# Block-sum transfers of a hybrid encoder layer moved from SyncE to GpSimd, and two stores made one

## The chip, the cores and the metric

One core of a Trainium2 chip runs the whole program. The time is the device time of one execution in microseconds; the median of the runs counts. All times that follow are in us.

## The reference

One encoder layer runs on two sequences (1024 and 2048 tokens of width 1024), each with 16 learned meta tokens ahead. Cut to what matters:

```
xn = rmsnorm(h, g_pre)
proj = xn @ w_in + b_in                      # 1024 -> 6672 columns
na_q, na_k, na_v, na_z, ml_qk, ml_v, ml_z, ml_o, ml_g, mg = split(proj)
ya = (neighbourhood_attention(na_q, na_k, na_v, na_rpb) * silu(na_z)) @ w_a
yb = (mlstm_both_directions(ml_qk, ml_v, ml_g, ml_o, ...) * silu(ml_z)) @ w_b
ga, gb = split(sigmoid(mg))
out = h + rmsnorm((ga * ya + gb * yb) @ w_out, g_post)
```

Inputs and outputs are float32, and so is the arithmetic.

## The kernel before

**Split products.** Each large product is made of float32r parts: a matrix is split into a high part (ScalarE's copy) and a low part (VectorE's subtraction of it), and a product takes three matmuls: high by high, high by low, low by high. Weights arrive in units of 128x1024; each becomes a pair `whi`, `wlo` in one of four buffers (`NBW`). The first time a unit is used it is loaded raw (`wraw`, L274), split, used, and both parts are stored to DRAM (L331); later uses load the two parts again (L296).

**Order of the work.** `PLAN` lists groups of projection columns by sequence and half: mLSTM, attention and gate columns of sequence 0 and of the two halves of sequence 1, then the final projections. The order of TensorE's instructions is written out by the program; the attention and the mLSTM of a sequence are interleaved with projections, so that TensorE always has a projection to work on. VectorE, ScalarE, GpSimd and SyncE are ordered by the scheduler, which goes by a simulated timeline. Each of the engines works its own list in that order; a transfer is issued by an instruction on one engine's list, and when that instruction waits (for its data, or for a semaphore), all that stands behind it on that engine waits too. SyncE issues nearly all transfers: loads of weights and of kept x, stores of projections, their reloads (`raw`, `va`, `um`), and the stores of kept weights.

**Block products.** For gate columns, and for the first twelve columns of the attention, pairs of 128 columns are computed by a seven-product (Strassen) scheme. Its inputs are block sums of weights and of x, made ahead, split in two parts each, and kept in DRAM:

- `wprep` (L564) makes the sums of weights of the eight pairs of gate columns. For each pair it loads two raw units into `pr` (L576), makes four pairs of sums in turn on VectorE, splits them with ScalarE and VectorE into `po`, and stores each sum (L594). `pr` and `po` have one buffer each.
- `nprep` (L600) does the same for the six pairs of attention columns, in tiles `xr` of a pool with four buffers: loads at L608, stores of the two parts of each sum at L623 and L624.
- `tprep` (L627) makes sums of x: `t0` to `t3`, each as a high and a low DRAM tile of 128x4x512, in four steps `e`. A step holds all four `xr` buffers. `t0` and `t1` are the two halves of one SBUF tile, and are made at once. For sequence 0 it also stores the scaled x itself (L653, `xkept`). The sums are stored at L667, a transfer of 128x512 for each sum, part and step.

These three are generators. `beside()` (L546), called after each piece of a projection, advances each of them every second to fourth turn, and ties the next piece behind VectorE's, ScalarE's and SyncE's last instructions of the projection, so that the sums are made in between. All of it runs in the first 1084 us of the profile. The readers come later: `tload` (L917) loads `t0` to `t3`, and the weight pump (L289) loads the sums of weights, both on SyncE; a semaphore makes them wait for the stores.

**Other lists.** GpSimd has 100 short instructions in the profile and a few transfers: the clearing of borders of `raw` (L1415), `st` and `ss` for the mLSTM, copies of meta keys, and loads of bias masks into `kx` (L1183), which ScalarE reads at L1192. Of the mLSTM, L1428 and L1503 are VectorE's convolution rows and the scaled key `kf`, which TensorE transposes at L1539; `L1520` is VectorE's scaling of values. The rows `pj` at L776 to L778 are projections whose stationary operand is a weight, those at L202 to L204 are those with x stationary or weight moving, all of them waiting for `whi` and `wlo`.

Of the kernel before, what the change touches and what calls it, by code (L numbers as in the profile page):

```python
# [10 lines left out]
F32 = mybir.dt.float32  # L11
# [7 lines left out]
P = 128  # L19
TCARGS = dict(schedule_with_timeline_sim=True)  # L20
D = 1024
# [32 lines left out]
PAIRS = [tuple(c[2 * p:2 * p + 2]) for c in (N_COLS, FM_COLS[24:]) for p in range(len(c) // 2)]  # L54
# [3 lines left out]
def _weight_units():  # L58

    return ([("i", x, P) for x in FM_COLS] + [("t", *c, a) for c in TM_COLS for a in range(2)]  # L60
            + [("m", f, P) for f in range(KT)] + [("o", c, a) for c in range(4) for a in range(2)])
# [76 lines left out]
class K:  # L138
# [425 lines left out]
    def wprep(self):  # L564

        nc = self.nc
        unit = {k: j for j, k in enumerate(_weight_units())}
        sub = lambda o, a, b: nc.vector.tensor_tensor(o, a, b, op=ALU.subtract)
        self.pq = ExitStack()
        pool = self.pq.enter_context(self.tc.tile_pool(name="pq", bufs=1, side="right", reuse_waits="tile"))  # L570
        for p in range(6, 14):
            if p == 10:
                [x for x in self.sides if x[0] is self.wside][0][1] = 4
            raw = pool.tile([P, 2, 2, 512], F32, name="pr", bufs=1)
            for f in range(2):
                nc.sync.dma_start(raw[:, f].rearrange("p a c -> p (a c)"), self.i["wu"][unit["i", PAIRS[p][f], P], :, :D])  # L576
            yield
            yield
            for f, ops in ((0, ("11", "12")), (1, ("21", "22")), (1, ("s3", "s1")), (0, ("s2", "s4"))):
                if ops[0] == "s3":  # L580
                    nc.vector.tensor_tensor(raw[:, 1, 1], raw[:, 1, 0], raw[:, 1, 1], op=ALU.add)
                    sub(raw[:, 1, 0], raw[:, 0, 0], raw[:, 1, 0])
                    yield
                if ops[0] == "s2":
                    sub(raw[:, 0, 0], raw[:, 1, 1], raw[:, 0, 0])
                    sub(raw[:, 0, 1], raw[:, 0, 1], raw[:, 0, 0])
                    yield
                o = pool.tile([P, 2, 2, 512], F32R, name="po", bufs=1)
                c = slice(p > 7 and ops[0] == "21", 2)
                nc.scalar.activation(o[:, c, 0], raw[:, f, c], AF.Copy)  # L590
                sub(o[:, c, 1], raw[:, f, c], o[:, c, 0].bitcast(F32))
                for q, op in list(enumerate(ops))[c]:
                    d = self.qd[p, op] = self.dp.tile([P, D], F32, name=f"q{p}{op}")
                    nc.sync.dma_start(d[:, :], o[:, q].rearrange("p a c -> p (a c)").bitcast(F32))  # L594
                yield
                yield
                if ops[0] == "11":
                    yield

    def nprep(self):  # L600

        nc = self.nc
        unit = {k: j for j, k in enumerate(_weight_units())}
        op = lambda o, a, b, x=ALU.subtract: nc.vector.tensor_tensor(o, a, b, op=x)
        for p in range(6):
            r0, r1 = [self.bp.tile([P, 2, 512], F32, name="xr", bufs=4) for _ in range(2)]
            for f, r in enumerate((r0, r1)):
                nc.sync.dma_start(r.rearrange("p a c -> p (a c)"), self.i["wu"][unit["i", PAIRS[p][f], P], :, :D])  # L608
            for _ in range(2):
                yield  # L610
            op(r1[:, 1], r1[:, 0], r1[:, 1], ALU.add)
            op(r1[:, 0], r0[:, 0], r1[:, 0])
            yield
            op(r0[:, 0], r1[:, 1], r0[:, 0])
            op(r0[:, 1], r0[:, 1], r0[:, 0])
            yield
            for r, ops in ((r1, ("s3", "s1")), (r0, ("s2", "s4"))):
                hi = self.bp.tile([P, 2, 512], F32, name="xr", bufs=4)
                nc.scalar.activation(hi.bitcast(F32R), r, AF.Copy)
                op(r.bitcast(F32R), r, hi)  # L620
                for q, o in enumerate(ops):
                    d = self.qd[p, o] = self.dp.tile([P, D], F32, name=f"q{p}{o}")
                    nc.sync.dma_start(d[:, :512], hi[:, q])  # L623
                    nc.sync.dma_start(d[:, 512:], r[:, q])  # L624
                yield

    def tprep(self, s, t0, after):  # L627

        nc, dp = self.nc, self.dp
        tt = lambda o, a, b, op=ALU.subtract: nc.vector.tensor_tensor(o, a, b, op=op)  # L630
        self.TD[s, t0] = [[dp.tile([P, 4, 512], F32, name=f"t{j}{part}{s}{t0}") for part in "hl"] for j in range(4)]
        td = self.TD[s, t0]
        while len(self.xs) < 2 or self.turn < after:
            yield
        if s == 0:
            for a in range(2):
                self.xkept[s, t0 + 512 * a] = [dp.tile([P, KT, 512], F32, name=f"x{part}{s}_{t0 + 512 * a}") for part in "hl"]
        halves = [[x[:, :, b:b + 512].bitcast(F32) for x in y] for y, b in zip(self.xs, (0 if s else NM, 0))]
        for e in range(4):
            ks = slice(2 * e, 2 * e + 2)  # L640
            r0, r1, ta, hi = [self.bp.tile([P, 2, 512], F32, name="xr", bufs=4) for _ in range(4)]
            for a, (r, (h, l)) in enumerate(zip((r0, r1), halves)):
                tt(r, h[:, ks], l[:, ks], ALU.add)
                if s == 0:
                    tt(r, r, self.rr[:, a:a + 1].to_broadcast([P, 2, 512]), ALU.mult)
                yield
            if s == 0:
                for a, r in enumerate((r0, r1)):
                    nc.scalar.activation(hi.bitcast(F32R), r, AF.Copy)
                    tt(ta.bitcast(F32R), r, hi)  # L650
                    for d, x in zip(self.xkept[s, t0 + 512 * a], (hi, ta)):
                        nc.sync.dma_start(d[:, ks, :], x)
                    yield  # L653
                    yield
            tt(ta[:, 0], r1[:, 0], r0[:, 0])
            tt(ta[:, 1], r1[:, 1], ta[:, 0])
            yield
            tt(r1[:, 0], r1[:, 1], r1[:, 0])
            tt(r0[:, 1], r0[:, 1], ta[:, 1])
            yield  # L660
            todo = [(hi, ta, (0, 1)), (r1[:, 1], r1[:, 0], (2,)), (r0[:, 0], r0[:, 1], (3,))]
            for a, b, js in todo:
                nc.scalar.activation(a.bitcast(F32R), b, AF.Copy)
                tt(b.bitcast(F32R), b, a)
                for q, j in enumerate(js):
                    for d, x in zip(td[j], (a, b)):
                        nc.sync.dma_start(d[:, e, :], x[:, q] if len(js) > 1 else x)  # L667
                yield


# [1492 lines left out]
```

## Time and profile before

| what | value |
|---|---|
| median of 3 runs | 2709.54 us (2709.08 to 2713.91) |
| profiled execution: its own time | 2707.9 us |
| its span | 2706.1 us |
| granted TensorE clock, mean | 0.992 |
| busy: TensorE, weight load, VectorE, ScalarE, GpSimd | 2647.0, 2336.6, 1943.8, 1439.9, 16.2 us |
| moved by DMA | 805.75 MB, mean 298 GB/s |
| queue q1 (SyncE), q0 (GpSimd) | 800.04 MB and 87.9%, 2.69 MB and 0.4% of the 16 DMA engines' time |

The span runs from the first to the last instruction of the profiled execution; its own time is 1.8 us longer. "Busy" counts the time in which an engine works on an instruction. The share of a DMA queue is the time that its packets took, as a share of the span of all 16 DMA engines. A row of a wait reads "who and where <- what it waited for". In a row of windows stand the window, its length, then busy time and count for TensorE, weight load, VectorE, ScalarE and GpSimd, then the granted clock, the DMA share and GB/s.

### The profile page before, as it was taken

The page shows a single profiled execution, that of the slowest core. Times are in us where ns is not written, and L with a number is a line of the kernel's source. Part 1 is how long each engine was busy: PE and PEld are TensorE (multiplying, and loading weights), DVE is VectorE, ACT ScalarE, POOL GpSimd, SP SyncE. Part 2 cuts the span into 40 slices and gives each one's busy share as a digit, 9 for nine tenths or more (in the row PEclk, how much of TensorE's full clock was granted, in tenths as well). Part 3 has the DMA queues.
Part 4 walks back from the last instruction along what each step waited for, and adds up shares of the span by engine and source line. Part 5 has one row for each costly group of instructions (what it writes and reads, how often), then busy time and mean ns, then how long its engine had stood idle before and what let it go on. Part 6 is the DMA issues. An engine that isn't in the chain of part 4 may idle for free.

```text
span 2706.1 us, 47482 instructions
## 1 busy us (share of the span) xinstructions
PE 2647.0 (98%) x15928; PEld 2336.6 (86%) x15928; DVE 1943.8 (72%) x5266; ACT 1439.9 (53%) x3388; POOL 16.2 (1%) x100
## 2 busy tenths in 40 slices
PE   9999899998999999999999999999999999999998
PEld 7998798898987999887888888888889998989888
DVE  5655588787766888545686776867478989898954
ACT  5433456554444655555665566656365666656521
POOL 0000000000000000000000000000000000000000
PEclk9999899998999999999999999999999999999999
DMA  9899886899978899878889998899899898898965
GB/s 366 336 342 335 309 306 233 299 336 327 348 228 285 294 320 314 274 265 276 259 271 332 370 297 264 279 331 363 274 305 314 259 309 278 282 305 260 324 238 203
DMA packets 411651, 805.75 MB, mean 298 GB/s; under 512 B 52016, under 2 KB 180992, under 8 KB 409104
## 3 DMA queue, kind: packets, MB, share of 16 engines
q1 hardware_dynamic: 410288, 800.04, 87.9%
q0 software_dynamic: 1120, 2.69, 0.4%
q8 instruction: 126, 2.06, 0.3%
q14 instruction: 117, 0.96, 0.1%
HBM read 548.96 MB, written 253.60 MB: 297 GB/s over the span
## 4 chain that ended last, share of the span: by engine, by line
PE 82%; DMA 9%; DVE 5%; ACT 2%; issue 1%; SPq 1%; DVEq 0%; ACTq 0%
PE pj L202 9%; PE pj L204 9%; PE pj L203 9%; PE pj L971 7%; PE pj L973 7%; PE pj L972 7%; PE pj L776 4%; PE pj L777 4%; PE pj L778 4%; PE pj L1918 3%; PE pj L1919 3%; PE pj L1920 3%; PE sm L1266 3%; PE tr L1251 2%; DMA wraw<-wu 2%
## 5 line engine op out<-in xcount | busy, mean ns | idle before, releaser
L202 PE MATMUL pj<-xh,whi 128*128 128x512 f32 (+1 forms) x896 | 345.5, 386 | 1.0 <-ACT whi L303 0.9
L204 PE MATMUL pj<-xh,wlo 128*128 128x512 f32 (+1 forms) x896 | 337.4, 377 | 5.7 <-DMA wlo<-wl 5.4
L203 PE MATMUL pj<-xl,whi 128*128 128x512 f32 (+1 forms) x896 | 337.9, 377 | 0.1
L776 PE MATMUL pj<-whi,xh 128*128 128x256 f32 (+1 forms) x1152 | 330.9, 287 | 6.8 <-DMA whi<-wh 6.8
L777 PE MATMUL pj<-wlo,xh 128*128 128x256 f32 (+1 forms) x1152 | 326.2, 283 | 3.7 <-DMA wlo<-wl 3.7
L778 PE MATMUL pj<-whi,xl 128*128 128x256 f32 (+1 forms) x1152 | 325.9, 283 | 0.0
L776 PEld LDWEIGHTS pj<-whi,xh 128*128 128x128 f32 x1152 | 218.6, 190 | 7.4 <-DMA whi<-wh 7.0
L777 PEld LDWEIGHTS pj<-wlo,xh 128*128 128x128 f32 x1152 | 218.3, 190 | 4.1 <-DMA wlo<-wl 4.0
L1918 PE MATMUL pj<-whi,mh 128*128 128x256 f32 x768 | 219.8, 286 | 0.5 <-DMA whi<-wh 0.5
L778 PEld LDWEIGHTS pj<-whi,xl 128*128 128x128 f32 x1152 | 218.3, 189 | 0.0
L1920 PE MATMUL pj<-whi,mlo 128*128 128x256 f32 x768 | 216.6, 282 | 0.0
L1919 PE MATMUL pj<-wlo,mh 128*128 128x256 f32 x768 | 216.6, 282 | 0.0
L204 PEld LDWEIGHTS pj<-xh,wlo 128*128 128x128 f32 x896 | 170.9, 191 | 38.8 <-DMA wlo<-wl 6.2
L202 PEld LDWEIGHTS pj<-xh,whi 128*128 128x128 f32 x896 | 170.9, 191 | 30.8 <-ACT whi L303 1.8
L203 PEld LDWEIGHTS pj<-xl,whi 128*128 128x128 f32 x896 | 170.9, 191 | 27.5 <-issue 1.0
L1258 DVE TENSOR_TENSOR pts<-tr,pts 96x384 fp32r<-96x384 f32 (+2 forms) x192 | 118.5, 617 | 57.2 <-ACT pts L1253 55.3
L1253 ACT ACTIVATE pts<-tr 96x384 fp32r<-96x384 f32 (+2 forms) x192 | 103.5, 539 | 98.8 <-PE tr L1251 98.1
L202 PE MATMUL pj<-yh,whi 128*128 128x512 f32 x384 | 154.4, 402 | 0.0
L203 PE MATMUL pj<-yl,whi 128*128 128x512 f32 x384 | 150.9, 393 | 0.8 <-DVE yl L1820 0.8
L204 PE MATMUL pj<-yh,wlo 128*128 128x512 f32 x384 | 151.1, 394 | 0.0
L1918 PEld LDWEIGHTS pj<-whi,mh 128*128 128x128 f32 x768 | 145.4, 189 | 1.5 <-DMA whi<-wh 0.7
L1919 PEld LDWEIGHTS pj<-wlo,mh 128*128 128x128 f32 x768 | 145.5, 189 | 0.8
(368 smaller groups left out, 6962.5 us busy)
## 6 DMA issues: line engine op xcount, KB each, us to landing
whi<-wh SPq DMA_DIRECT2D x136, 512.0 KB
wlo<-wl SPq DMA_DIRECT2D x136, 512.0 KB
whi<-q SPq DMA_DIRECT2D x62, 512.0 KB
wlo<-q SPq DMA_DIRECT2D x50, 512.0 KB
wraw<-wu SPq DMA_DIRECT2D x48, 512.0 KB
gt<-st SPq DMA_DIRECT2D x96, 256.0 KB
tg<-gt SPq DMA_DIRECT2D x96, 256.0 KB
wh<-whi SPq DMA_DIRECT2D x36, 512.0 KB
```

What stands on the lines that cost most here:

```text
L202: mm(out, ah, bh, start=start, stop=False)
L203: mm(out, ah, bl, start=False, stop=False)
L204: mm(out, al, bh, start=False, stop=stop)
L776: nc.tensor.matmul(o, xh, wh, start=k == 0, stop=False)
L777: nc.tensor.matmul(o, xh, wl, start=False, stop=False)
L778: nc.tensor.matmul(o, xl, wh, start=False, stop=k == KT - 1)
L971: mm(bank, w[:, 0, k], xh[:, k], start=fresh and k == 0, stop=False, skip_group_check=True)
L972: mm(bank, w[:, 0, k], xl[:, k], start=False, stop=False, skip_group_check=True)
L973: mm(bank, w[:, 1, k], xh[:, k], start=False, stop=k == 3, skip_group_check=True)
L1918: nc.tensor.matmul(o, mh[:, k, xs], wh, start=clear > 0 and k == 0, stop=False)
L1919: nc.tensor.matmul(o, mh[:, k, xs], wl, start=False, stop=False)
L1920: nc.tensor.matmul(o, ml[:, k, xs], wh, start=False, stop=clear < 2 and k == KT - 1)
```

## The change

Six calls that issue transfers in `wprep`, `nprep` and `tprep` go from `nc.sync` (SyncE) to `nc.gpsimd`: the raw weights, the sums of weights, the kept x, and the sums of x. Apart from that, `t0` and `t1` become one DRAM tile of 128x2x4x512 for each part, and the two halves made at once are stored by one transfer of 256 rows.

```diff
 # wprep
-nc.sync.dma_start(raw[:, f].rearrange("p a c -> p (a c)"), self.i["wu"][unit["i", PAIRS[p][f], P], :, :D])
+nc.gpsimd.dma_start(raw[:, f].rearrange("p a c -> p (a c)"), self.i["wu"][unit["i", PAIRS[p][f], P], :, :D])
...
-nc.sync.dma_start(d[:, :], o[:, q].rearrange("p a c -> p (a c)").bitcast(F32))
+nc.gpsimd.dma_start(d[:, :], o[:, q].rearrange("p a c -> p (a c)").bitcast(F32))
 # nprep
-nc.sync.dma_start(r.rearrange("p a c -> p (a c)"), self.i["wu"][unit["i", PAIRS[p][f], P], :, :D])
+nc.gpsimd.dma_start(r.rearrange("p a c -> p (a c)"), self.i["wu"][unit["i", PAIRS[p][f], P], :, :D])
...
-nc.sync.dma_start(d[:, :512], hi[:, q])
-nc.sync.dma_start(d[:, 512:], r[:, q])
+nc.gpsimd.dma_start(d[:, :512], hi[:, q])
+nc.gpsimd.dma_start(d[:, 512:], r[:, q])
 # tprep
-self.TD[s, t0] = [[dp.tile([P, 4, 512], F32, name=f"t{j}{part}{s}{t0}") for part in "hl"] for j in range(4)]
-td = self.TD[s, t0]
+t01 = [dp.tile([P, 2, 4, 512], F32, name=f"t01{part}{s}{t0}") for part in "hl"]
+td = {j: [dp.tile([P, 4, 512], F32, name=f"t{j}{part}{s}{t0}") for part in "hl"] for j in (2, 3)}
+self.TD[s, t0] = [[t[:, 0] for t in t01], [t[:, 1] for t in t01], td[2], td[3]]
...
-nc.sync.dma_start(d[:, ks, :], x)
+nc.gpsimd.dma_start(d[:, ks, :], x)
...
-for q, j in enumerate(js):
-    for d, x in zip(td[j], (a, b)):
-        nc.sync.dma_start(d[:, e, :], x[:, q] if len(js) > 1 else x)
+for q, x in enumerate((a, b)):
+    nc.gpsimd.dma_start(t01[q][:, :, e, :] if len(js) > 1 else td[js[0]][q][:, e, :], x)
```

SyncE's list has 2514 transfers before and 2268 after, GpSimd's 14 and 236. TensorE's list is the same in both.

SyncE's list around the loads of one kept weight pair, before (the pair that TensorE reads at 637.75 in the profile; `gg` and `to` are stores of the projection, `va` loads values of the mLSTM, `xh` and `xl` store kept x of sequence 1):

```order
L551 DMA xh_512_5787<-xh 128x512
L576 DMA pr<-wu 128x1024 x2
L551 DMA xl_512_5788<-xl 128x512
L1476 DMA va_3219<-mv_246 128x2x128
L667 DMA t3h_5889<-xr 128x512
L296 DMA whi<-wh_1478 128x1024
L667 DMA t3l_5890<-xr 128x512
L667 DMA t2h_5887<-xr 128x512
L816 DMA gg_259<-stT 128x2x16
L819 DMA to_257<-stT 128x2x248
L667 DMA t2l_5888<-xr 128x512
L296 DMA wlo<-wl_1479 128x1024
```

and the same place of SyncE's list in the changed kernel:

```order
L816 DMA gg_259<-stT 128x2x16
L551 DMA xh_512_5777<-xh 128x512
L551 DMA xl_512_5778<-xl 128x512
L819 DMA to_257<-stT 128x2x248
L296 DMA whi<-wh_1474 128x1024
L296 DMA wlo<-wl_1475 128x1024
L1476 DMA va_3209<-mv_246 128x2x128
```

The two loads now stand one behind the other; the raw weights and the sums of x between them are gone from this list, and `va` stands behind the pair.

GpSimd's list at the same place in the changed kernel; before, no transfer stood between this clearing of `raw` and the next:

```order
L667 DMA t3l_5878<-xr 128x512
L1415 MEMSET raw 128x1
L594 DMA q12s_7197<-po 128x1024
L594 DMA q12s_7199<-po 128x1024
L576 DMA pr<-wu 128x1024 x2
L667 DMA t01h_5873<-xr 256x1x512
L667 DMA t01l_5874<-xr 256x1x512
L667 DMA t3h_5877<-xr 128x512
L667 DMA t3l_5878<-xr 128x512
```

The raw weights, the sums of weights and the sums of x stand here in one list, the clearing of `raw` between them, and `t01` goes in one row where `t0` and `t1` had two.

VectorE's list ahead of the `kf` that TensorE waits for at L1539, before:

```order
L1428 SCALAR_TENSOR_TENSOR cv<-raw,cw,cv 128x256
L568 TENSOR_TENSOR po<-pr,po 128x2x512
L1520 SCALAR_TENSOR_TENSOR vwl<-va_3220,g_wT_3173,vwh 128x130
L1520 SCALAR_TENSOR_TENSOR vwl<-va_3220,g_wT_3177,vwh 128x130
L1520 SCALAR_TENSOR_TENSOR vwl<-va_3220,g_wT_3173,vwh 128x130
L1520 SCALAR_TENSOR_TENSOR vwl<-va_3220,g_wT_3177,vwh 128x130
L1503 SCALAR_TENSOR_TENSOR kf<-th,cv 128x256
```

and in the changed kernel:

```order
L1428 SCALAR_TENSOR_TENSOR cv<-raw,cw,cv 128x256
L1520 SCALAR_TENSOR_TENSOR vwl<-va_3210,g_wT_3163,vwh 128x130
L1520 SCALAR_TENSOR_TENSOR vwl<-va_3210,g_wT_3167,vwh 128x130
L1520 SCALAR_TENSOR_TENSOR vwl<-va_3210,g_wT_3163,vwh 128x130
L1520 SCALAR_TENSOR_TENSOR vwl<-va_3210,g_wT_3167,vwh 128x130
L568 TENSOR_TENSOR po<-pr,po 128x2x512
L1503 SCALAR_TENSOR_TENSOR kf<-th,cv 128x256
```

The low part of a sum of weights (L568, written from `pr` into `po`) moved behind the four scalings of values; both stand ahead of `kf`, as before.

## Prediction

> **What bounds the kernel now.** I read the page first, then TensorE's waits, then the stretches around those waits by windows and rows. The page:
>
> ```profile
> span 2706.1 us, 47482 instructions
> PE 2647.0 (98%) x15928; PEld 2336.6 (86%) x15928; DVE 1943.8 (72%) x5266; ACT 1439.9 (53%) x3388; POOL 16.2 (1%) x100
> ...
> q1 hardware_dynamic: 410288, 800.04, 87.9%
> q0 software_dynamic: 1120, 2.69, 0.4%
> ```
>
> TensorE is busy for 2647.0 of 2706.1 us. TensorE's instructions are the same in both kernels, in the same order, so its work stays; a gain comes only out of the 59.1 us of idle time and out of a lower granted clock. Nearly everything moved by DMA goes over q1, SyncE's queue. GpSimd (q0) carries 2.69 MB of 805.
>
> Who lets TensorE wait, longest first; columns: total us, times, longest:
>
> ```profile
> PE tr L1539 <- DVE kf L1503: 11.7, 2, 8.9
> PE pj L776 <- DMA whi<-wh: 6.8, 1, 6.8
> PE sm L204 <- DVE ktl L1543: 6.4, 6, 2.8
> PE pj L204 <- DMA wlo<-wl: 5.4, 2, 2.8
> PE pj L777 <- DMA wlo<-wl: 3.7, 1, 3.7
> ```
>
> Waits for weight loads add up to 6.8+5.4+3.7 = 15.9 us. TensorE's own rows give their places: 637.75 and 642.00 (one weight pair, 10.5 us), 760.19, and 817.22.
>
> ```profile
> 637.75 0.58 PE L776 MATMUL pj<-whi,xh 128*128 128x256 f32 x1 [6.83 <-DMA whi<-wh]
> 642.00 0.58 PE L777 MATMUL pj<-wlo,xh 128*128 128x256 f32 x1 [3.66 <-DMA wlo<-wl]
> 760.19 0.65 PE L204 MATMUL pj<-xh,wlo 128*128 128x512 f32 x1 [2.53 <-DMA wlo<-wl]
> 817.22 0.50 PE L204 MATMUL pj<-xh,wlo 128*128 128x512 f32 x1 [2.83 <-DMA wlo<-wl]
> ```
>
> Now the same place by windows (busy us and counts by engine, then granted clock, share of the 16 DMA engines, GB/s):
>
> ```profile
> 600.00:620.00 20.00, 20.00 (x167) 20.00 (x166) 17.78 (x37) 11.54 (x26) 0.10 (x1) 1.00 0.97 340
> 620.00:640.00 20.00, 11.51 (x92) 11.01 (x90) 10.28 (x27) 7.47 (x17) 0.00 (x0) 0.85 1.02 354
> 640.00:660.00 20.00, 18.00 (x131) 18.00 (x132) 12.27 (x40) 6.83 (x18) 0.00 (x0) 0.81 0.99 352
> 740.00:760.00 20.00, 17.66 (x124) 15.92 (x122) 9.55 (x31) 7.04 (x20) 0.00 (x0) 1.00 0.85 283
> ```
>
> Two things stand there. The stall costs more than its length: the clock falls to 0.85 and 0.81, and from 620 to 660 TensorE makes 223 matmuls where 334 fit at the pace of the window before, so 111/167 x 20 = **13.3 us** are lost for 10.5 us of waiting. And the DMA engines' share is 0.97 to 1.02: the loads are late while the engines have no room. SyncE's chain shows how a load waits its turn (start, us, what):
>
> ```profile
> 628.09 7.30 DMA xl<-xl
> ...
> 635.46 0.33 SPq L667
> 635.79 0.05 issue
> 635.84 6.11 DMA wlo<-wl
> ```
>
> The store issued at 635.46 is the eighth after the load issued at 628.09, and starts when that one has landed (628.09 + 7.30 = 635.39). SyncE has eight DMA semaphores in turn, so **eight transfers in flight** are its limit; the weight load wlo stands behind that store.
>
> **The change part by part.** It moves 246 transfers: wprep 16 loads and 58 stores, nprep 12 and 48, tprep 16 of kept x and 96 sums, of which pairing makes 72. GpSimd then has eight semaphores of its own. Everything moved lies before 1084 us; behind it nothing changes.
>
> *1. The pair at 637 to 642.* If lanes were what is short, all 13.3 us would go. But lanes only matter while the engines have room, and they have next to none from 560 on. Their listing from 560 to 640:
>
> ```profile
> q1 hardware_dynamic: 15904, 28.92, 101.1%
> ...
> q12s<-po SPq DMA_DIRECT2D x4, 512.0 KB
> ...
> pr<-wu SPq DMA_DIRECT2D x2, 512.0 KB
> ...
> q<-po SPq DMA_DIRECT2D x1, 512.0 KB
> ...
> t0h<-xr SPq DMA_DIRECT2D x2, 256.0 KB
> ```
>
> With the seven other groups like t0h (16 stores in all), that is 7 x 0.524 + 16 x 0.262 = 7.9 MB moved out of 28.9. Those bytes still pass through the same engines ahead of the weights: their data is ready no later than in SyncE's order, so whoever issues them, the pair lands when the sum of bytes is done. Taken out of the sum: 0 us, with -13.3 as the bound if lanes decide after all.
>
> What the moved bytes cost by the other queue is bounded from two rows. Over the page, q0 takes 0.004 x 2706.1 x 16 / 2.69 = 64 us of an engine per MB, and q1 0.879 x 2706.1 x 16 / 800.04 = 48. In the most crowded stretch, 900 to 1090, it is nearly even:
>
> ```profile
> q1 hardware_dynamic: 32723, 59.94, 94.4%
> q0 software_dynamic: 160, 0.43, 0.7%
> ```
>
> 0.944 x 3040 / 59.94 = 48 and 0.007 x 3040 / 0.43 = 49.5. So a moved MB costs 1.5 to 16 us more; I take 8, between them, as both shares are rounded to a digit: 7.9 x 8 / 16 = **+4 us** at this stall (bounds +0.7 and +8). Closing the gaps in the engines' share (0.97 of 600 to 620, 0.99 behind) gives back some 3% of 60 us: **-2**.
>
> *2. The wait at 760.* Here the share is 0.85: SyncE, not the engines, is behind, still with rows of the crowded stretch. Fewer transfers on it should take this 2.5 us away: **-2** (bounds -2.5 and 0). The wait at 817 comes long after wprep's last store, whose row is
>
> ```profile
> L594 SPq DMA_DIRECT2D q13s<-po x4: 326/430/952, 710.3 to 728.0; - x4
> ```
>
> so I put 0 there, with its own 2.8 us as the bound below.
>
> *3. Issue on GpSimd.* Its transfers of 64 partitions:
>
> ```profile
> L1183 POOL DMA_DIRECT2D kx<-masks x10: 509/513/779, 802.6 to 2423.7; - x10
> ```
>
> Half a microsecond each; one of 128 partitions is not shown and lies between 0.5 and 1.0 us, a pair of 256 rows up to 2. 222 new ones at 0.5 to 1.1 are 110 to 245 us in 1024; GpSimd's 1% hides that. What stands behind a waiting store on GpSimd are memsets of raw, st and ss and the loads of kx. One of each with its reader, a transfer and a ScalarE row:
>
> ```profile
> 581.62 0.10 POOL L1415 MEMSET raw<- 128x1 f32 x1 [46.63 <-DVE cv L1428]
> ...
> 593.08 0.46 SPq L1416 DMA_DIRECT2D raw<-mq  x1
> ...
> 1002.62 0.52 POOL L1183 DMA_DIRECT2D kx<-masks  x1 [199.00 <-PE sm L1220]
> ...
> 1022.13 0.89 ACT L1192 ACTIVATE kd<-kx 64x832 fp32r<-64x832 f32 x1
> ```
>
> That leaves 11 us for the memset, and 19 for kx, its landing among them. So 0 us; +5 if one kx load comes after its reader.
>
> The Trainium skill, DMA: Bandwidth & Descriptors, section SWDGE vs HWDGE vs iDMA, says that these descriptors are written to SBUF by GpSimd, which VectorE can lock out there. By that rule the issues would stretch while VectorE works; the row above, 509 to 779 ns with VectorE at 72%, shows almost none of it, and the trace differs from a large effect.
>
> *4. The stretch 900 to 1090,* where nprep's 60 transfers move:
>
> ```profile
> 900.00:1090.00 190.00, 188.54 (x1517) 185.70 (x1516) 154.19 (x374) 105.62 (x220) 1.03 (x2) 1.00 0.96 319
> ```
>
> TensorE waits for no DMA there now. Moved are 12 x 0.524 + 48 x 0.262 + 14 x 0.262 = 22.6 MB; at +8 us per MB and engine that is 11 us of lateness spread over 190, hidden by weights loaded ahead. I put **+2** on it (0 to +11 if that cover goes).
>
> *5. Order.* VectorE and ScalarE get po and xr rows a few places earlier or later; the 8.9 us wait at L1539 stays, since kf stands behind the same rows in both orders. 0, plus or minus 3.
>
> Sum: +4 - 2 - 2 + 2 = +2 on the execution's own 2707.9 us. The median of the runs is 2709.54, 1.6 above it: **2711.5 us**, no change within 0.2% (5.4 us, about what a measurement of this kernel can tell).
>
> **Rivals.**
>
> *Lanes decide (faster).* Between the issues of the pair's whi and wlo SyncE puts three stores of t among five transfers; the first two rows:
>
> ```profile
> 631.03 0.47 SPq L296 DMA_DIRECT2D whi<-wh  x1
> 631.66 0.35 SPq L667 DMA_DIRECT2D t3l<-xr  x1
> ```
>
> Then come t2h, gg, to and t2l, and wlo only at 635.84. The three go away. If the weight loads pass because fewer transfers share eight lanes, and the gaps in the engines' share are the lanes' doing, the stall goes with its clock: -13.3, -2.5 at 760, 2709.5 - 16 = 2694. For it: 8 in flight is the limit shown in the chain. Against it: a share of 1.02 at 637. Chance 0.28.
>
> *The second queue goes first (slower).* If the engines take from both queues in turn, a weight load on q1 waits for q1's rows ahead and for everything that GpSimd has issued meanwhile, also what SyncE's order had put behind it. In 560 to 640 about 27% of the bytes are moved; stores ready within the 7 us that a load takes, 0.27 x 350 GB/s x 7 us = 0.7 MB, pass ahead and cost 2 us at each tight load. With the upper price per MB: +8 + 2 at 642, its clock loss in proportion (13.3/10.5), and as much as 4 in 900 to 1090: 2709.5 + 12.7 + 4 = 2726. It decides once a moved MB costs over some 12 us more, or the pair's wait passes 14 us. For it: no room at 637. Against it: 49.5 against 48 per MB in the crowded stretch. Chance 0.32.
>
> The Trainium skill, DMA: Bandwidth & Descriptors, section Queues, rings and completion order, states that each engine goes round-robin between queues a packet at a time; by that rule this rival's sharing holds, and no run here shows it, as q0 holds 0.4%.
>
> *The change does nothing it says.* GpSimd's rows in the changed kernel do hold the transfers, so no chance apart.
>
> **How the numbers follow.** No change 0.40, lanes 0.28, second queue 0.32. Range: the two rivals' times are its ends, as each leaves about a tenth outside: 2694 to 2726. Faster by over 0.2%: 0.27; within: 0.40; slower: 0.33.
>
> **What will show it.** q0 with about 94 MB; its us per MB against 48 tells the price. The wait at L776/L777 near 640: present and 8 to 15 us long (mine), gone (lanes), longer (second queue). The wait at 760 gone. POOL busy 120 to 260 us. New rows "PE <- DMA whi" between 900 and 1100 would prove item 4 wrong. A gain or loss behind 1100 us would prove the whole sum wrong.

## The result and the profile after

The changed kernel takes 2704.67 us, the median of 12 runs (2700.61 to 2709.02); the kernel before, run beside it, 2713.25 (12 runs, 2707.77 to 2723.17). The ratio is **0.9968 (0.9954 to 0.9982)**: 0.3% faster. The forecast was no change at 2711.5, within 0.2%; the time is inside its range of 2694 to 2726, but lower than "no change".

The two profiled executions don't show it: the spans are 2706.1 and 2706.9 us. A second execution of each, traced later on one chip, has 2713.8 and 2699.5. So each kernel has two traces here, and a term is only as good as the two agree. The page of after:

```profile
PE 2645.3 (98%) x15928; PEld 2334.8 (86%) x15928; DVE 1941.2 (72%) x5266; ACT 1442.0 (53%) x3388; POOL 140.0 (5%) x322
...
q1 hardware_dynamic: 374864, 708.79, 79.0%
q0 software_dynamic: 26944, 93.93, 9.4%
```

91 MB have gone to q0. What they cost on each queue is told by what q1 lost and q0 gained. On q1 they took (0.879 x 2706.1 - 0.790 x 2706.9) x 16 / 91.24 = 42 us of an engine per MB, on q0 they take (0.094 x 2706.9 - 0.004 x 2706.1) x 16 / 91.24 = 43: the moved bytes are not dearer. (The 48 of q1 as a whole is the mean over other transfers too.) TensorE's waits after, the first four (total us, times, longest), and its rows at the two places of the prediction:

```profile
PE tr L1539 <- DVE kf L1503: 14.5, 2, 8.9
PE pj L204 <- DMA wlo<-wl: 6.2, 2, 3.7
PE pj L776 <- DMA whi<-wh: 5.9, 1, 5.9
PE pj L202 <- DMA whi<-wh: 4.7, 1, 4.7
```

```profile
638.86 0.58 PE L776 MATMUL pj<-whi,xh 128*128 128x256 f32 x1 [5.86 <-DMA whi<-wh]
640.15 0.58 PE L777 MATMUL pj<-wlo,xh 128*128 128x256 f32 x1 [0.71 <-DMA wlo<-wl]
757.08 0.77 PE L202 MATMUL pj<-xh,whi 128*128 128x512 f32 x1 [4.69 <-DMA whi<-wh]
761.95 0.79 PE L204 MATMUL pj<-xh,wlo 128*128 128x512 f32 x1 [3.68 <-DMA wlo<-wl]
```

At 640 the wait for `whi` stays and the one for `wlo` goes from 3.66 to 0.71 us; near 757 a wait for `whi` is new, and the one for `wlo` longer. The windows of after, in the columns of before:

```profile
620.00:640.00 20.00, 13.58 (x109) 13.08 (x107) 13.15 (x34) 10.39 (x26) 3.26 (x6) 0.90 1.00 359
640.00:660.00 20.00, 19.85 (x146) 19.85 (x147) 14.27 (x49) 8.53 (x23) 1.07 (x2) 0.85 1.02 372
740.00:760.00 20.00, 13.58 (x85) 11.46 (x83) 9.79 (x38) 8.55 (x22) 0.00 (x0) 0.88 0.82 270
```

TensorE's order is the same in all kernels here, so the time from one matmul to another can be set side by side. In us, with TensorE's waits in brackets; the bounds are those of the first trace of before:

| stretch | before | before, 2nd | after | after, 2nd | what differs |
|---|---|---|---|---|---|
| 308 to 345 | 37.5 (3.9) | 36.5 (3.1) | 38.3 (5.8) | 37.2 (5.0) | `kf` near 328 later |
| 600 to 660 | 59.9 (10.5) | 57.6 (8.6) | 57.4 (7.5) | 55.0 (5.8) | `wlo` |
| 690 to 712 | 22.0 (2.8) | 20.4 (2.6) | 19.0 (0.9) | 19.0 (0.9) | `ktl` of VectorE |
| 740 to 770 | 30.2 (2.5) | 34.2 (5.9) | 36.7 (8.4) | 34.5 (5.5) | `whi`, `wlo` near 757 |
| 1060 to 1090 | 30.1 (0.7) | 33.8 (2.9) | 29.2 (0.0) | 29.5 (0.0) | `yg` of VectorE |
| whole span | 2706.1 | 2713.8 | 2706.9 | 2699.5 | |

By the means, the change gains 2.6 at the pair, 2.2 at 690, 2.7 at 1060, and loses 0.8 at 328 and 3.4 at 757: 3.2 of the 6.8 us between the means of the spans. These sizes are rough, as two traces of one kernel differ by up to 4.0 us in a stretch: at the pair the nearest traces of the two kernels have 57.6 and 57.4, at 757 34.2 and 34.5, and at 328 they overlap. The other 3.6 lie in no place that stands out. About 3 of them are behind 1090, where the prediction allowed nothing; there before has 1615.9 and 1619.3, after 1615.8 and 1613.2, so the first traces agree and two traces of one kernel differ as much. Whether that part belongs to the change is not shown.

### The profile page after: what moved, and what is told of

Same layout as the page of the kernel before. It is cut to its first block, busy times and chain, and to the rows that moved or that the text cites. A ratio compares the mean times of both kernels' runs of the same rounds, so it can differ in the third digit from the quotient of the medians.

```text
span 2706.9 us, 47551 instructions
## 1 busy us (share of the span) xinstructions
PE 2645.3 (98%) x15928; PEld 2334.8 (86%) x15928; DVE 1941.2 (72%) x5266; ACT 1442.0 (53%) x3388; POOL 140.0 (5%) x322
## 4 chain that ended last, share of the span: by engine, by line
PE 82%; DMA 10%; DVE 5%; ACT 1%; issue 1%; SPq 0%; DVEq 0%; ACTq 0%
PE pj L202 9%; PE pj L204 9%; PE pj L203 9%; PE pj L971 7%; PE pj L973 7%; PE pj L972 7%; PE pj L776 4%; PE pj L777 4%; PE pj L778 4%; PE pj L1919 3%; PE pj L1918 3%; PE pj L1920 3%; PE sm L1266 3%; PE tr L1251 2%; DMA wlo<-wl 1%
```

## Experiments

All ratios are to runs of before on the same chip, with 95% intervals. Four groups of kernels.

**The same kernels again, and the two halves of the change.** No edit in the first two. The third keeps the pairing and issues everything from SyncE, the fourth the reverse:

```diff
 # e3_pair: tprep of the changed kernel
-nc.gpsimd.dma_start(t01[q][:, :, e, :] if len(js) > 1 else td[js[0]][q][:, e, :], x)
+nc.sync.dma_start(t01[q][:, :, e, :] if len(js) > 1 else td[js[0]][q][:, e, :], x)
 # e4_queue: tprep of before, with
-nc.sync.dma_start(d[:, e, :], x[:, q] if len(js) > 1 else x)
+nc.gpsimd.dma_start(d[:, e, :], x[:, q] if len(js) > 1 else x)
```

> The kernel before, unchanged, as the measure of this size of difference: ratio 1.000, within 0.999 to 1.001, by every theory. Its trace is a second execution of before: if the waits for the weight pair at L776/L777 near 640 us are again about 10 us with a clock of 0.81 to 0.85 behind them, they are fixed in the program; if they differ by several us between the two traces of before, they vary from one execution to the next, and one profile of each kernel can't carry a gain of 0.3%.

Measured 1.0000 (0.9988 to 1.0012). The pair's wait is 5.0 + 3.6 us against 6.8 + 3.7 in the first trace, so it stays; near 757 it is 5.9 against 2.5, so single places vary by 3 us.

> The changed kernel again, on the chip on which before is run too. Theory A (SyncE's shorter list and its eight semaphores let the weight loads go sooner): ratio 0.996 to 0.998, and in the trace the waits of TensorE for whi and wlo come to less than in the trace of before on this chip. Theory B (nothing is gained; the earlier difference belongs to the chip or to the single execution): ratio 0.999 to 1.001.

Measured 0.9976 (0.9965 to 0.9986). Theory B falls. Theory A's sign holds, not its reason: TensorE's waits for `whi` and `wlo` in its projections come to 13.7 us, against 17.6 in before's second trace, but the first traces have 17.5 for after and 15.9 for before.

> Pairing alone: t0 and t1 are stored by one transfer, and every transfer stays on SyncE, which has 24 transfers fewer. Theory A: it is a tenth of the relief of SyncE's list (24 of 246), so ratio 0.999 to 1.000. Rival C (the pairing is what gains, since a pair takes one semaphore and one issue where the stores of t stand ahead of the weight loads): ratio 0.996 to 0.998.

Measured 0.9972 (0.9963 to 0.9981): 24 transfers fewer give as much as the whole change. Rival C has the number, but its reason is only part of it, since SyncE's list is also in another order:

```profile
627.46 2.57 SPq L576 DMA_DIRECT2D pr<-wu  x2
630.07 0.51 SPq L551 DMA_DIRECT2D xl<-xl  x1
630.62 0.43 SPq L296 DMA_DIRECT2D whi<-wh  x1
631.10 0.88 SPq L296 DMA_DIRECT2D wlo<-wl  x1
```

The stores of t2 and t3, of which before has three between `whi` and `wlo`, are issued from 632.99 on, behind the pair. TensorE waits 4.65 us for `whi` and 0.70 for `wlo`, with no transfer on GpSimd.

> The queue alone: all these transfers on GpSimd, t0 and t1 stored apart as before (246 transfers moved). Theory A: as the changed kernel, ratio 0.996 to 0.998. Rival C (the pairing gains): 0.999 to 1.001. Theory B: 0.999 to 1.001 for this, the pairing and the whole.

Measured 0.9953 (0.9940 to 0.9966): without the pairing the change is better. Gains in proportion to what leaves SyncE's list are out, and the two halves don't add. In the trace about 5 us come from the stretch 20 to 308, where the whole change gains nothing; the cause is told under e6.

**Each helper alone, and another queue.** The edit is in each case the `gpsimd` of the changed kernel in one function of before (`wprep`, `tprep`, `nprep`); in e8 all three with `nc.scalar`.

> Only wprep's 74 transfers on GpSimd; those of x and of the attention's weights stay on SyncE. Theory L (the place of a load in SyncE's list decides: taken-out rows let wlo near 640 go sooner): ratio 0.998 to 0.999, wait for wlo at L777 near 640 at 0.7 to 3.7 us, a part of the relief. Theory S (stores issued by a second queue overtake SyncE's loads while the DMA engines are full): the loss of the whole change at 328 us (5 us wait of L1539 instead of 2.8) and near 757 (waits for whi and wlo of 5.5 to 8.4 us together instead of 2.5 to 5.9) comes from wprep's stores, and shows here too. Theory R (before has an unlucky order near 640 and 757, and any reshuffle of SyncE's list ends it): ratio about 0.997, as with the pairing alone.

Measured 0.9975 (0.9962 to 0.9988), the ratio of theory R. `wlo` at 640 waits 0.7 us; near 757 TensorE waits 7.1, near 328 5.3, at the places that theory S named. Whether the stores are to blame is asked by e13.

> Only tprep's transfers on GpSimd, with the pairing (88 transfers for 112). Theory L: ratio 0.996 to 0.998, wait for wlo at L777 near 640 at 0.7 us, 2.9 less than before; the wait of L1539 at 328 stays at 2.8 us, since wprep's stores stand behind the values' loads again. Theory S: no loss at 328, a loss near 757 only if the sums of x are stored there. Theory R: 0.997.

Measured **0.9944** (0.9930 to 0.9959), better than the whole and than every range. The pair's `wlo` is as theory L has it, and `whi` and `wlo` near 750 wait 0.4 us together. But some 5.5 us come from a place that no theory had, the stretch before 308. VectorE's rows there, of before and of this kernel:

```profile
299.68 0.17 DVE L358 TENSOR_SCALAR ss<-ss 128x4 f32<-128x4 f32 x1 [1.63 <-ACT xsq L355]
...
302.05 1.23 DVE L304 TENSOR_TENSOR wlo<-wraw,whi 128x1024 fp32r<-128x1024 f32 x1
...
307.23 0.42 DVE L1503 SCALAR_TENSOR_TENSOR kf<-th,cv 128x256 f32<-128x256 f32 x1
```

```profile
299.72 1.06 DVE L1428 SCALAR_TENSOR_TENSOR cv<-raw,cw,cv 128x256 f32<-128x256 f32 x2
301.26 0.43 DVE L1503 SCALAR_TENSOR_TENSOR kf<-th,cv 128x256 f32<-128x256 f32 x1 [0.48 <-ACT th L1430]
```

In before, an inverse square root of the next half (L358, then eleven rows of 0.2 us) and a split stand ahead of `kf`, for which TensorE waits 8.9 us; here they stand behind it, and TensorE waits 1.1. The changed kernel has before's order at this place. In e4 TensorE waits 2.6 us there, also with the inverse square root behind `kf`.

> Only nprep's 60 transfers on GpSimd, which lie behind 830 us. Theory L: the wait at 1078 to 1081 for yg L1281 (0.7 and 2.9 us in two traces of before, none in the changed kernel) goes: ratio 0.9985 to 0.9995, and nothing changes ahead of 830. Theory R: nothing near 640 and 757 is reshuffled, so ratio 0.9995 to 1.0005. If it is 0.997, all the places that I named are wrong.

Measured 0.9992 (0.9982 to 1.0002); the wait for `yg` is gone, and with it 0.9 to 4.7 us of that stretch. So the gain there belongs to nprep. It is VectorE's order again: in before's second trace `yg` stands behind nprep's rows of L604, in the changed kernel ahead of the same:

```profile
1076.68 1.82 DVE L604 TENSOR_TENSOR xr<-xr 128x512 f32<-128x512 f32 x2
1078.54 0.28 DVE L1281 TENSOR_TENSOR yg<-sm,yg 64x128 f32<-64x128 f32 x1
```

```profile
1074.79 0.60 DVE L1281 TENSOR_TENSOR yg<-sm,yg 64x128 f32<-64x128 f32 x2
...
1075.55 0.69 DVE L604 TENSOR_TENSOR xr<-xr 128x512 f32<-128x512 f32 x1
```

> The changed kernel with all these transfers issued by ScalarE instead of GpSimd: a hardware queue as SyncE's is, sharing its eight semaphores. The pairing stays. Theory L: near 640 as the changed kernel (wlo 0.7 us), ratio 0.997 to 0.999, with something lost where ScalarE's own work waits behind an issue of about 0.4 us or for a semaphore. Theory S: the losses at 328 and near 757 appear here as in the changed kernel, since the sharing of engines is the same; if they are gone, they belong to the software queue or to the freedom of eight more semaphores. Theory that lanes decide: with no semaphores added nothing is gained beyond the pairing's 0.9972, and TensorE's waits for weights are as in the pairing alone.

Measured 1.0093 (1.0077 to 1.0108), slower than any theory had it. TensorE reaches the pair 6 to 7 us later than in before, finds `whi` there, and starts on `wlo` at 639.15 after a wait of 1.2. ScalarE's own work pays: 830 to 1060 takes 254.4 us instead of 229.9, with waits for `prb` and `kth` behind its issues. It doesn't tell lanes from list, since TensorE comes late to both places.

**The mechanisms by themselves.** e9 is the changed kernel with wprep as before; e10 moves wprep's loads (L576) only; e11 is the changed kernel with the stores of L835 moved too; e12 is e6 with each store of a sum of x issued twice:

```diff
 # e10_prload, to before
-nc.sync.dma_start(raw[:, f].rearrange("p a c -> p (a c)"), ...)
+nc.gpsimd.dma_start(raw[:, f].rearrange("p a c -> p (a c)"), ...)
 # e11_nv, to the changed kernel
-nc.sync.dma_start(dst, st[r * 64:r * 64 + 64, a, :wd])
+nc.gpsimd.dma_start(dst, st[r * 64:r * 64 + 64, a, :wd])
 # e12_double, to e6_tprep; z01 and z are tiles like t01 and td
 nc.gpsimd.dma_start(t01[q][:, :, e, :] if len(js) > 1 else td[js[0]][q][:, e, :], x)
+nc.gpsimd.dma_start(z01[q][:, :, e, :] if len(js) > 1 else z[js[0]][q][:, e, :], x)
```

> tprep (paired) and nprep on GpSimd, wprep left on SyncE: the whole change without its 74 wprep transfers. If the parts add, 0.9944 x 0.9992 = 0.9936, the wait for yg L1281 near 1066 (3.9 us with tprep alone) gone, and TensorE's waits for whi and wlo near 750 under 1 us as with tprep alone. If the order that the scheduler happens to find decides more than the queues do, anything from 0.993 to 0.998, and the terms do not add.

Measured **0.9934** (0.9922 to 0.9946), close to the product of the two parts (0.9936), and it beats both kernels. By places they add only in part: the wait for `yg` is gone, and 1060 to 1090 takes 29.2 us instead of e6's 34.8, but near 747 TensorE waits 3.0 us for `whi` and `wlo`, not under 1, and 740 to 770 takes 30.8 instead of 26.3. That the ratio fits so well is partly luck.

> Only the 16 loads of raw gate weights (L576) on GpSimd, the smallest change of SyncE's list that can be made in this place: 8.4 of 800 MB. Theory L (gain in proportion to what leaves SyncE's list): ratio 0.9995 to 1.0005. Theory R (any reshuffle of the scheduler's order ahead of 760 us ends the long pair wait near 640, as 24 transfers fewer did by 0.28%): 0.997 to 0.998.

Measured 0.9972 (0.9960 to 0.9984), by 16 loads. TensorE's rows at the pair, and the issues:

```profile
633.75 0.39 PE L776 MATMUL pj<-whi,xh 128*128 128x256 f32 x1 [1.03 <-DMA whi<-wh]
635.08 0.39 PE L777 MATMUL pj<-wlo,xh 128*128 128x256 f32 x1 [0.94 <-DMA wlo<-wl]
```

```profile
613.79 1.06 POOL L576 DMA_DIRECT2D pr<-wu  x2 [1.50 <-DVE kl L1631]
```

```profile
627.88 0.51 SPq L296 DMA_DIRECT2D whi<-wh  x1
628.43 0.85 SPq L296 DMA_DIRECT2D wlo<-wl  x1
```

The pair waits 2.0 us instead of 10.5 and 8.6, and the clock stays at 1.00 from 620 to 660. TensorE's waits for `kf` near 308 (8.8) and for `yg` (2.8) are as in before. Two things differ at the pair. In before the two raw loads (1.05 MB) were issued at 626.60 and 627.17, right ahead of the pair, though the last row that reads their buffer (L568) ends at 611.55; on GpSimd they go at 613.79, half a microsecond after that row's end there (613.22). And `whi` and `wlo` stand one behind the other, ahead of t3 and t2, as in e3. e3 has the second without the first, and tells them apart: the new order takes the wait for `wlo` from 3.6 and 3.7 to 0.7, and with the raw loads away too the wait for `whi` falls from e3's 4.65 to 1.03. So theory R has the ratio, and the reshuffle is part of the cause, but not all: the list also held back loads that could go, until they were in the way.

> The changed kernel, and the stores of attention values at L835 on GpSimd as well. Between 735 and 757 us these are about half of SyncE's rows, each issued some 12 us after its data is ready, and the loads of the weight pair of 757 stand behind them. If SyncE's backlog sets the wait near 757 (5.5 and 8.4 us for whi and wlo in two traces of the changed kernel), it falls under 2 us and the ratio is 0.995 to 0.9965. If the DMA engines set it, it stays, and the ratio is 0.997 to 0.998.

Measured **0.9938** (0.9924 to 0.9951), lower than both ranges, and TensorE waits for no load between 740 and 760:

```profile
740.00:760.00 20.00, 20.00 (x104) 16.63 (x103) 12.45 (x47) 11.44 (x34) 2.24 (x4) 1.00 0.64 240
```

SyncE issues this `whi` at 735.73 here and at 751.18 in the changed kernel, where the engines' share is 0.82, so they have room there too. The wait near 757 is SyncE's backlog. The stores of L835 are not the only way to end it: in e6 and e13 SyncE keeps them, issues `whi` at 741.61 and 744.23, and TensorE waits 0.4 us and nothing.

> tprep on GpSimd as in the run before, and every store of a sum of x issued a second time, to a DRAM tile that nobody reads: 25 MB more by GpSimd's queue, some 4 MB of them between 560 and 640. If the DMA engines' room sets the landing of the pair near 632 (my prediction's step 1), the wait at L776 grows by up to 4 MB x 3 us = 12 us from 6.0, and the ratio is above 1.000. If SyncE's list and its semaphores set it, the wait stays within 2 us of 6.0 and the ratio at 0.994 to 0.997.

Measured 1.0090 (1.0076 to 1.0103). The pair:

```profile
651.05 0.58 PE L779 MATMUL pj<-whi,xh 128*128 128x256 f32 x1 [13.95 <-DMA whi<-wh]
653.70 0.58 PE L780 MATMUL pj<-wlo,xh 128*128 128x256 f32 x1 [2.07 <-DMA wlo<-wl]
```

e6's 6.0 + 0.7 has become 14.0 + 2.1. SyncE issues `whi` here at

```profile
636.36 1.39 SPq L296 DMA_DIRECT2D whi<-wh  x1
```

so it is under way for 14.7 us, until 651.05, where e6's takes 6.7 (625.28 to 631.93); TensorE is some 11 us later here than in e6 too. The queues from 630 to 651 (packets, MB, share of 16 engines):

```profile
q0 software_dynamic: 1190, 4.09, 51.8%
q1 hardware_dynamic: 2454, 3.82, 50.7%
```

The engines are full, and half of them works for GpSimd. Bytes do set when the pair lands, and those of the other queue count although they were issued beside it.

**Why is the whole change at 0.997, when parts of it reach 0.993?** e13 has only wprep's stores (L594) on GpSimd, e14 the changed kernel without them, e15 is e9 with L835 moved.

> Only wprep's 58 stores of sums of weights (L594) on GpSimd; its 16 loads of raw weights stay on SyncE, the rest is as before. If the loads are what gains in wprep's part and the stores what loses (the 16 loads alone gave 0.9972, loads and stores 0.9975 with 7 us of waits for whi and wlo near 757), ratio 0.999 to 1.002, and the pair wait near 640 is 8 us or more. If the stores gain too, 0.997 to 0.998.

Measured 0.9958 (0.9942 to 0.9975): a miss. The pair waits 9.7 us, as said; but near 757 nothing waits, and `kf` near 308 waits 3.3. Moved alone, the stores lose nothing, and theory S's reading of e5 falls.

> The changed kernel with wprep's 58 stores back on SyncE: loads of raw weights, nprep and tprep (paired) on GpSimd. VectorE's inverse square root (L358) stands behind the first two kf rows here, as in the kernels that wait 1 to 3 us at L1539 near 308, where before and the changed kernel wait 8.9. If wprep's stores are what the whole change loses by, ratio 0.990 to 0.9935, and the pair wait near 632 under 3 us. If the sums of x on the second queue hold the pair up by themselves, that wait stays at 5 to 6 us and the ratio is 0.9925 to 0.9945.

Measured **0.9931** (0.9913 to 0.9948), the lowest, not told apart from 0.9934 and 0.9938. TensorE waits 2.9 + 1.6 us at the pair, 0.8 near 750, and for `kf` 5.2 and 1.3, where the changed kernel waits 8.9 and 5 to 5.7. Against the mean of the changed kernel's two traces the stretches 600 to 660, 740 to 770 and 20 to 345 are 3.7, 8.9 and 7.7 us shorter, more than the 13.5 between the spans (2689.7 against 2703.2); smaller losses come behind. The ratio is in the range for "wprep's stores are what the whole change loses by", the pair's wait of 4.5 is not under its 3 us, and e13 has the stores alone gain. So they cost the whole change something only together with the other transfers; why is not shown.

> tprep (paired), nprep and the stores of attention values (L835) on GpSimd, wprep on SyncE: the two best pieces together. If what they gain adds, the 3.0 us of waits near 747 of the former go and the ratio is 0.9915 to 0.993, under both kernels and under the 0.9934 and 0.9938 of the pieces. If it stays at 0.9934, the stores at L835 gain only where wprep's transfers are on GpSimd too.

Measured 0.9944 (0.9924 to 0.9964): it doesn't add. The waits near 747 are gone, but `ktl` waits 1.9 us and `kth` 1.9 near 710, with the clock lost behind them.

## Why the prediction was wrong, point by point

Two steps failed: at the pair, the premise that the order of issue gains nothing, and the term for VectorE's order, which was put at nothing. All three terms that were not zero (the pair, 760, 900 to 1090) came out with the opposite sign. That the time lies inside the range is therefore luck.

**1. The pair (+4 - 2).** The step that failed is the premise that the pair lands "when the sum of bytes is done", "whoever issues them", so that nothing could be gained by the order of issue. The half of it that is about bytes holds: in e12 more bytes delay the pair. The half about order does not. Where three stores of t are issued between `whi` and `wlo`, TensorE waits 3.7 and 3.6 us for `wlo` (before), 4.3 (e7) and 4.1 (e13); where the two loads are neighbours it waits 0.7 in both traces of the changed kernel, and 0.7 in e3, in which SyncE still issues every byte. So this gain is the order of SyncE's list, and needs no second queue.

For `whi` nothing was gained in the changed kernel, in a way that the prediction had only as a rival. SyncE's and GpSimd's issues of after around `whi`:

```profile
624.67 2.01 SPq L296 DMA_DIRECT2D whi<-wh  x1
626.93 1.58 SPq L296 DMA_DIRECT2D wlo<-wl  x1
```

```profile
624.81 0.56 POOL L667 DMA_DIRECT2D t3h<-xr  x1 [2.97 <-ACT xr L664]
```

```profile
626.93 13.17 DMA wlo<-wl
```

`whi` goes 6.4 us earlier than before (631.03), `wlo` 8.9 (635.84), but `wlo` is under way for 13.17 us instead of 6.11. The queues of after from 618 to 630 say why:

```profile
q0 software_dynamic: 936, 3.42, 72.8%
q1 hardware_dynamic: 1641, 1.24, 31.3%
```

GpSimd's transfers take nearly three quarters of the engines, while SyncE's loads creep. From 626.93 to 640, while `wlo` is under way, q0 still has 35.2% and q1 63.3%. That is the rival "the second queue goes first", and its price is what eats the earlier issue. The Trainium skill, DMA: Bandwidth & Descriptors, section Queues, rings and completion order, has the engines go from queue to queue by packets; the trace agrees that neither queue waits for the other to be empty, and does not show the turns. What is left is `wlo`, on which TensorE starts 1.3 us after `whi` instead of 4.2. The dearer bytes, +4, are nothing: 42 us of an engine per MB on q1, 43 on q0, so the row of the crowded stretch (49.5 against 48) was a better guide than the page's 64. The term measured -2.6 for +2. Without the dearer bytes, the +4 here and the +2 of point 4, the sum would have been -4, or 2705.5, close to the measured time, but not by the places where the time was gained.

**2. The wait at 760 (-2)** became +3.4 by the means. Its cause was read rightly, "SyncE, not the engines, is behind"; e11 shows it. But fewer transfers on SyncE did not shorten the backlog here: the stores of L835 stand around this pair in SyncE's list, and they stayed.

**3. Issue on GpSimd (0)** was right: 140.0 us busy, and TensorE's waits name no memset of `raw` and no `kx`. Two issues of 128x1024 take 1.18 us:

```profile
616.22 1.18 POOL L594 DMA_DIRECT2D q12s<-po  x2 [1.35 <-DVE po L568]
```

**4. 900 to 1090 (+2)** measured -2.7, at `yg`. What TensorE stops waiting for there is a row of VectorE whose place changed. A transfer stands behind it: in before, the sums of L604 ahead of that `yg` wait for nprep's own load, here in the first trace:

```profile
1070.73 0.69 DVE L604 TENSOR_TENSOR xr<-xr 128x512 f32<-128x512 f32 x1 [1.17 <-DMA xr<-wu]
```

So VectorE's order made TensorE wait for a load that it does not need.

**5. Order (0, plus or minus 3)** was the mis-sized term. In the changed kernel it is -2.2 at `ktl` and the same -2.7 at `yg`, -4.9 in all. At `ktl` a sum of x of 1.22 us, with others behind it, stands ahead in before and behind in after; e5 has the same 19.0 us in this stretch as after, so it comes with wprep's part:

```profile
701.65 1.22 DVE L630 TENSOR_TENSOR xr<-xr 128x1024 fp32r<-128x1024 f32 x1
...
705.82 0.42 DVE L1543 TENSOR_TENSOR ktl<-tr,kth 128x256 fp32r<-128x256 f32 x1
```

```profile
702.49 0.42 DVE L1543 TENSOR_TENSOR ktl<-tr,kth 128x256 fp32r<-128x256 f32 x1
702.83 1.22 DVE L630 TENSOR_TENSOR xr<-xr 128x1024 fp32r<-128x1024 f32 x1
```

Near 328 TensorE waits 2.8 us for `kf` in both traces of before, 5.7 and 5.0 in after. That is mostly no VectorE order: SyncE issues the load of values (`va`), whose scaling (L1520) stands ahead of that `kf`, 6 us later, behind its own backlog. The rest is order: four more scalings, 1.2 us, stand ahead of `kf` in after. The row of `va` in before and in after:

```profile
313.26 0.37 SPq L1476 DMA_DIRECT2D va<-mv  x1
```

```profile
319.35 0.37 SPq L1476 DMA_DIRECT2D va<-mv  x1
```

In e4, e6, e9, e13, e14 and e15 the stretch 20 to 308 gives 5 to 8 us. "kf stands behind the same rows in both orders" was true of the changed kernel and is why it has none of these.

**The rivals.** "Lanes decide" gave 2694 with the pair's wait gone. The sign is right, and it had seen the three stores between the two loads, but the wait for `whi` stays in the changed kernel, and e3 gains at `wlo` with no semaphore added. Whether a semaphore or a place in the list held a row ahead of `whi` was not separated: e8 was to do that and didn't. "The second queue goes first" is shown by e12 and by the shares above; its total had the wrong sign, since the gains at other places are larger.

**What stays open** is why the ratios of the parts multiply in e9 and not in the whole, and where 3.6 of the 6.8 us come from. The first is located (308, 640, 757) but not derived: moving a transfer changes the simulated times from which the scheduler orders VectorE and SyncE, and which order comes out was seen only by building the kernel.

## What to carry to other kernels

In a kernel whose lists are ordered by a scheduler, a change of queue is first a change of order on all engines: compare the rows ahead of each engine that TensorE waits for, at every wait of some us, and give that term a range as large as those waits. A second queue lets a load go early that an in-order list holds back, which is worth having for loads without hurry (16 loads gave what 222 transfers did, part of it by the order that came with them); large stores issued beside full engines overtake the loads that are urgent. Move what stands ahead of the urgent load, or between two that are needed together, in its own list, and look at the share of each queue in the microseconds of the wait.

## What the runs showed of the hardware

- With transfers outstanding on both queues, GpSimd's got 72.8% of the engines from 618 to 630 in the changed kernel, with 936 packets for 3.42 MB, against 31.3% for SyncE's 1641 packets of 1.24 MB. The shares are not fixed: from 630 to 651 in e12 they were 51.8 and 50.7%.
- A long wait at TensorE goes with a lower granted clock: 0.85 and 0.81 in the two windows from 620 to 660 of before with waits of 10.5 us, 1.00 in those of e10 with 2.0 us, and 0.57 from 640 to 660 in e12, where the wait of 14 us ends at 651.05:

```profile
640.00:660.00 20.00, 6.88 (x39) 6.59 (x40) 2.45 (x7) 2.90 (x7) 0.13 (x1) 0.57 1.04 395
```

- The price of a MB was the same by the queues of three engines that moved the same bytes: in e8 ScalarE's took 0.089 x 2732.3 x 16 / 91.24 = 43 us of an engine, as GpSimd's in the changed kernel (43) and SyncE's in before (42):

```profile
q10 hardware_dynamic: 35040, 91.24, 8.9%
```
